# First ada scale on VectorE, 1/rms rows behind the first products, a later scatter, unheld splits at five seams

## The chip, the cores and the metric

One core of one Trainium2 chip runs the program. The metric is the device time of one execution in microseconds (us); lower is better. The kernel computes in single precision: each product of a weight matrix is made of three products of reduced-precision parts (high x high, high x low, low x high), so each weight tile is first split into a high part (a cast on ScalarE, ACT) and a low part (a subtraction on VectorE, DVE).

## The reference, cut to what matters

256 tokens of 1024 features pass through two stacks, one behind the other.

```python
def first_block(x, c, ...):
    for layer in range(2):
        sh1, sc1, g1, sh2, sc2, g2 = split(ada_mod(c, ada_w[layer], ada_b[layer]), 6)   # silu(c) @ w + b
        h = rmsnorm(x, norm_mix_g[layer]) * (1.0 + sc1) + sh1
        y = mlstm_mixer(h, ...) if layer < 1 else stick_breaking_mixer(h, ...)
        x = x + g1 * y
        h = rmsnorm(x, norm_ffn_g[layer]) * (1.0 + sc2) + sh2
        x = x + g2 * peer_ffn(h, ...)          # top 16 of 16384 experts in 8 heads
    return x

def second_block(h, p, ...):
    for i in range(2):
        h = h + 0.5 * swiglu(rms_norm(h, g_ffn1[i]), ffn1_w_in[i], ffn1_w_out[i])
        hn = rms_norm(h, g_mix[i])
        h = h + (mla_mixer(hn, ...) if i == 0 else fox_mixer(hn, ...))
        h = h + 0.5 * swiglu(rms_norm(h, g_ffn2[i]), ffn2_w_in[i], ffn2_w_out[i])
        gate = sigmoid(rms_norm(h, g_ple[i]) @ ple_w_gate[i])
        h = h + gate * (p[i] @ ple_w_proj[i])
    return h
```

## The kernel before, in words

**Stages.** The list at L1731 gives the order: mlstm, peer(0), stick, peer(1), then ffn1_0, mla, ffn2_0 with ple(0), ffn1_1, fox, ffn2_1 with ple(1). A seam is the border between two of them: the residual x is finished there, normalised, transposed and split for the next stage. The program hands instructions to a scheduler that sets the order on each engine by its own estimates. Two things constrain it: `issue_after` (an instruction is issued only behind another; here "hold"), and `pe_order`, in which TensorE's instructions keep the order of the code.

**Start.** `ada_first` (L585) makes the first shift and scale: vectors of 1024, silu(c) times two 1024x1024 blocks of `ada_w`. Eight loads of 1 MB come from SP's queue, first the four of the shift (pool "first"), then the four of the scale (`wpool`, whose four buffers serve all later weights). TensorE multiplies them with `cs` as a one-column stationary operand (L601), the result row is copied (L606), turned into columns of 128 by transposes (L608), and the bias added (L615, L612, L613). Until both are there the transposed, normalised x cannot be scaled and shifted (L332, L334).

**Weights.** `units` and `stream` (L191 to L211) load 128x2048 tiles named raw; `split` (L216) makes whi (L229) and wlo (L230). `lin_s` (L274) makes 24 products of 128x256 from one unit (lines L280 to L282), `lin_m` (L234) products of 128x512 (L244 to L246).

**Late normalisation.** In the second block the products start with the unnormalised x times the gain. `head` transposes x (L306) and splits it (xhi L323, xlo L324); `norm_late` (L402) works out 1/rms on DVE (L408, L346 to L355). Where the 1/rms is wanted along the columns, it multiplies the identity by it (rrt, L422), a product with ones spreads it (L423), and ACT copies the result (rrow, L424). `ffn` (L1150) runs over 22 chunks: gate and up products of one chunk (24 + 24), then sg = gate x rrow (L1182), its silu (L1183), up x rrow (L1184), and the second product two chunks behind. `fox` (L1092) uses the row for its forget gates (L1116 to L1124), whose sums are transposed on TensorE (L1122).

**Seams.** `tail` and `lin_m(tail=True)` write the last products, the evacuations (`residual`: x at L467, L469) and the heads in `pe_order`; then `boundary` (L477) puts up to five holds on the next stage's first splits: the first `free` of them wait for the last addition to x, the others for the last xlo. `free` is 2 for mla and fox, 1 for the ffn stages, and 5 (no hold) from ffn2 to ple. ple(l) evacuates through ACT (L1226) and DVE (L1227, L1228).

**Scatter.** In a peer layer TensorE runs "u phase" units (L1468, 32 products each) while DVE picks the experts. `par(u0, 7, (rt, 15))` at L1589 runs seven units beside the routing; the scatter of the chosen weights starts with products L1360 on ex (L1355). Later in the phase a set of indices passes through jT (L1700).

Of the kernel before, what the change touches and what calls it, by code (L numbers as in the profile page):

```python
# [10 lines left out]
F32 = mybir.dt.float32  # L11
# [6 lines left out]
OP = mybir.AluOpType  # L18
AX = mybir.AxisListType

P = 128
S = 256
D = 1024
NK = D // P
# [91 lines left out]
class Kern:  # L116
    def __init__(self, ctx, tc, I, out):
# [12 lines left out]
        self.early = True  # L130
# [4 lines left out]
        self.free = 1  # L135
# [98 lines left out]
    def lin_m(self, xT, nk, srcs, ncol, evac, tag="acc", blocks=None, tail=False, late=0):  # L234
# [24 lines left out]
        if tail:  # L259
            rest = [(k, next(us)) for k in range(4, nk, kk)]  # L260
            with self.pe_order():
# [7 lines left out]
                if late:  # L269
                    self.holds = [(), self.evac_ins, self.evac_ins]  # L270
                else:
                    self.boundary()
# [129 lines left out]
    def norm_late(self, rows=False, inv=False):  # L402
# [8 lines left out]
        R = None  # L411
        if rows:
            self.uid += 1
            R = self.spool.tile([P, S], F32, tag="rrow", bufs=1, name=f"rrow_{self.uid}")
            ps = self.ps("acc")
            for tb in range(2):
                t = self.spool.tile([P, P], F32, tag="rrt", bufs=2, name=f"rrt_{self.uid}_{tb}")
                r = rs[tb]
                if inv:
                    r = self.small(1, "rms")  # L420
                    nc.vector.reciprocal(r, rs[tb])
                nc.vector.tensor_scalar(t, self.ident, r, None, OP.mult)  # L422
                nc.tensor.matmul(ps[:, tb * P:(tb + 1) * P], self.ones, t, start=True, stop=True)  # L423
            nc.scalar.copy(R, ps[:, 0:S])  # L424
        return hT, rs, R

# [7 lines left out]
    def tail(self, prod, ev, acc):  # L434

        with self.pe_order():
# [13 lines left out]
            self.boundary()  # L450
# [68 lines left out]
    def ada_sum(self, src, bias, out):  # L519
# [4 lines left out]
        sm = self.small(NK, "adsm")  # L524
        for h in range(2):
            ps = self.ps("acc" if self.early else "mm")
# [10 lines left out]
        nc.vector.tensor_add(out, sm, bias)  # L537
# [47 lines left out]
    def ada_first(self):  # L585
# [3 lines left out]
        row = [self.ps("acc") for _ in range(4)]  # L589
        ctx = ExitStack()  # L590
        pool = ctx.enter_context(self.tc.tile_pool(name="first", bufs=4, side="right", reuse_waits="tile"))
        for e in range(2):
            for k0 in range(0, NK, 2):
                self.uid += 1
                raw = (self.wpool if e else pool).tile([P, 2048], F32, tag="raw", bufs=4, name=f"raw_{self.uid}")
                nc.sync.dma_start(raw.rearrange("p (k n) -> p k n", k=2),
                                  self.I["ada_w"][0, k0 * P:(k0 + 2) * P, e * D:(e + 1) * D].rearrange("(k p) n -> p k n", p=P))
                for k in range(k0, k0 + 2):
                    for h in range(2):
# [1283 lines left out]
```

## Time and profile before

| | |
|---|---|
| median of 3 runs | 2852.85 us (2849.33 to 2853.03) |
| profiled execution | 2852.44 us, span 2850.7 us |
| mean granted clock of TensorE | 0.987 of full speed |
| TensorE (PE) | 2754.4 us busy |
| weight loads (PEld), beside PE | 2537.3 us |
| DVE | 1931.0 us |
| ACT | 929.4 us |
| POOL | 433.2 us |
| read from HBM | 743.76 MB, 261 GB/s |

The span is what the profiler saw from the first to the last instruction; the time of the execution is a little longer. Busy times are sums over the span, and say nothing on which engine ends a stage; the waits and the windows do. The granted clock is the share of full speed that TensorE was given in a stretch.

### The profile page before, as it was taken

The numbers are of one execution on the slowest core, as the hardware profiler recorded it, in microseconds if no ns is written. First come the engines' busy times: TensorE is split into PE (matmuls) and PEld (weight loads), VectorE is DVE, ScalarE is ACT, GpSimd is POOL, SyncE is SP. The second block draws the span as 40 slices with busy tenths as digits, with TensorE's granted clock in tenths as the row PEclk, the third lists the DMA queues.
The fourth block names the chain that finished last, engine by engine and source line by source line (L and its number), as shares of the span: only waits on it lengthen the run. The fifth ranks groups of instructions, "written<-read, shape, count | busy, mean of one in ns | idle before, by whom it ended". The sixth has DMA issues, their size and how long they took to land.

```text
span 2850.7 us, 47773 instructions
## 1 busy us (share of the span) xinstructions
PE 2754.4 (97%) x19250; PEld 2537.3 (89%) x19250; DVE 1931.0 (68%) x4005; ACT 929.4 (33%) x1728; POOL 433.2 (15%) x445
## 2 busy tenths in 40 slices
PE   7999999999998999999999998999999999999999
PEld 4789999999998779999999997998799889887998
DVE  4877866768545977867777446667666666666665
ACT  3653111100001664111100003446654554456444
POOL 0000342333332000233443430000000000000000
PEclk9999999999999999999999999999999999999999
DMA  7654999999997724899999996554255545442553
GB/s 263 225 196 167 346 397 356 372 378 384 380 409 310 264 102 147 314 375 415 412 408 407 408 408 244 182 186 154 73 192 192 182 163 192 154 157 92 190 187 113
DMA packets 155582, 747.92 MB, mean 262 GB/s; under 512 B 15696, under 2 KB 17360, under 8 KB 111840
## 3 DMA queue, kind: packets, MB, share of 16 engines
q1 hardware_dynamic: 93984, 527.93, 49.9%
q0 software_dynamic: 58752, 213.94, 19.2%
q10 hardware_dynamic: 2624, 3.00, 0.4%
q8 instruction: 151, 2.47, 0.4%
q14 instruction: 71, 0.58, 0.1%
HBM read 743.76 MB, written 1.05 MB: 261 GB/s over the span
## 4 chain that ended last, share of the span: by engine, by line
PE 68%; DMA 17%; DVE 9%; issue 3%; ACT 2%; POOL 1%; ACTq 0%; DVEq 0%; POOLq 0%
PE ps_acc L1519 11%; PE ps_mm L280 7%; PE ps_mm L282 7%; PE ps_mm L281 7%; PE ps_mm L1468 6%; DMA raw<-in_peer_v_dram 5%; DMA row<-in_peer_un_dram,ix 5%; DMA row<-in_peer_v_dram,ix 4%; PE ps_acc L245 4%; PE ps_acc L244 4%; PE ps_acc L246 4%; PE ps_acc L1161 3%; PE ps_acc L1163 3%; PE ps_acc L1162 3%; DMA row<-in_ada_w_dram 2%
## 5 line engine op out<-in xcount | busy, mean ns | idle before, releaser
L230 DVE TENSOR_TENSOR wlo<-raw,whi 128x1024 fp32r<-128x1024 f32 (+1 forms) x440 | 533.2, 1214 | 237.3 <-ACT whi L229 228.8
L229 ACT CAST whi<-raw 128x1024 fp32r<-128x1024 f32 (+1 forms) x440 | 455.3, 1042 | 509.5 <-PE ps_mm L281 244.4
L1519 PE MATMUL ps_acc<-X,raw 128*128 128x176 f32 (+1 forms) x4096 | 606.4, 308 | 10.4 <-DMA raw<-in_peer_v_dram 10.0
L1468 PE MATMUL ps_mm<-hT,raw 128*128 128x176 f32 (+1 forms) x4096 | 604.6, 309 | 4.5 <-ACT jT L1700 4.3
L1519 PEld LDWEIGHTS ps_acc<-X,raw 128*128 128x128 f32 x4096 | 587.0, 190 | 16.3 <-DMA raw<-in_peer_v_dram 14.9
L1468 PEld LDWEIGHTS ps_mm<-hT,raw 128*128 128x128 f32 x4096 | 590.4, 191 | 6.2 <-ACT jT L1700 4.6
L280 PE MATMUL ps_mm<-xhi,whi 128*128 128x256 f32 (+1 forms) x1488 | 422.7, 284 | 11.4 <-DVE sg L1182 7.4
L281 PE MATMUL ps_mm<-xlo,whi 128*128 128x256 f32 (+1 forms) x1488 | 420.0, 283 | 2.0 <-DVE xlo L324 1.1
L282 PE MATMUL ps_mm<-xhi,wlo 128*128 128x256 f32 (+1 forms) x1488 | 420.0, 283 | 0.3 <-DVE wlo L230 0.3
L1438 DVE SCALAR_TENSOR_TENSOR sacc<-row,dots,sacc 128x1024 f32<-128x1024 f32 x172 | 220.8, 1284 | 146.5 <-DMA row<-in_peer_v_dram,ix 145.9
L280 PEld LDWEIGHTS ps_mm<-xhi,whi 128*128 128x128 f32 (+1 forms) x1488 | 282.7, 190 | 17.0 <-DVE sg L1182 8.3
L1421 DVE SCALAR_TENSOR_TENSOR row<-row,hn 128x1024 f32<-128x1024 f32 x176 | 213.4, 1224 | 113.6 <-DMA row<-in_peer_un_dram,ix 113.3
L1414 POOL DMA_INDIRECT row<-in_peer_un_dram,ix x176 | 199.3, 1132 | 588.0 <-DVE ti L1619 240.1
L281 PEld LDWEIGHTS ps_mm<-xlo,whi 128*128 128x128 f32 (+1 forms) x1488 | 282.3, 190 | 6.3 <-DVE xlo L324 1.8
L282 PEld LDWEIGHTS ps_mm<-xhi,wlo 128*128 128x128 f32 (+1 forms) x1488 | 282.9, 190 | 1.3 <-DVE wlo L230 0.8
L1414 POOL DMA_INDIRECT row<-in_peer_v_dram,ix x176 | 190.1, 1080 | 337.0 <-ACT ix L1411 171.1
L1470 ACT ACTIVATE X<-ps_mm 128x352 f32<-128x352 f32 (+1 forms) x128 | 57.5, 451 | 482.0 <-PE ps_mm L1468 384.9
L1411 ACT CAST ix<-ps_mm 128x4 int32<-128x4 f32 x88 | 14.2, 161 | 492.8 <-PE ps_mm L1408 336.1
L1161 PE MATMUL ps_acc<-whi,ah 128*128 128x512 f32 x352 | 139.3, 396 | 0.0
L1163 PE MATMUL ps_acc<-whi,al 128*128 128x512 f32 x352 | 137.8, 392 | 0.0
L1162 PE MATMUL ps_acc<-wlo,ah 128*128 128x512 f32 x352 | 136.8, 389 | 0.0
L1508 DVE SCALAR_TENSOR_TENSOR X<-ps_mm,X 128x128 f32<-128x128 f32 (+1 forms) x210 | 66.2, 365 | 85.2 <-PE ps_mm L1502 64.3
(466 smaller groups left out, 3764.6 us busy)
## 6 DMA issues: line engine op xcount, KB each, us to landing
raw<-in_ffn_dram SPq DMA_DIRECT2D x132, 1024.0 KB, 4.9
raw<-in_peer_u_dram SPq DMA_DIRECT2D x128, 1024.0 KB, 8.2
raw<-in_peer_v_dram SPq DMA_DIRECT2D x128, 1024.0 KB, 13.1
raw<-in_ada_w_dram SPq DMA_DIRECT2D x28, 1024.0 KB, 5.3
row<-in_ada_w_dram POOLq DMA_DIRECT2D x40, 512.0 KB, 10.4
raw<-in_peer_wq_dram SPq DMA_DIRECT2D x16, 1024.0 KB, 5.5
raw<-in_fox_in_dram SPq DMA_DIRECT2D x12, 1024.0 KB, 5.0
raw<-in_ma_vo_dram SPq DMA_DIRECT2D x8, 1024.0 KB, 5.0
```

Source lines behind the costliest of these rows:

```text
L229: nc.scalar.copy(hi[:, 0:u], raw)
L230: nc.vector.tensor_sub(lo[:, 0:u], raw, hi[:, 0:u])
L280: nc.tensor.matmul(o, wh, xh[:, k, :], start=(k == 0), stop=False)
L281: nc.tensor.matmul(o, wh, xl[:, k, :], start=False, stop=False)
L282: self.last_mm = nc.tensor.matmul(o, wl, xh[:, k, :], start=False, stop=(k == NK - 1))
L1161: nc.tensor.matmul(o, ah[:, t], wh[:, n], start=(c == 0), stop=False)
L1162: nc.tensor.matmul(o, ah[:, t], wl[:, n], start=False, stop=False)
L1163: nc.tensor.matmul(o, al[:, t], wh[:, n], start=False, stop=(c == FFC - 1))
L1414: nc.gpsimd.indirect_dma_start(row, None, src, bass.IndirectOffsetOnAxis(held["ix"][:, k:k + 1], 0))
L1438: nc.vector.scalar_tensor_tensor(sacc[u], row, w, sacc[u], OP.mult, OP.add)
L1468: self.last_mm = nc.tensor.matmul(ps[:, i * TD:(i + 1) * TD], raw[:, o:o + P], hT[:, k, TS:S], start=(k == 0), stop=(k == NK - 1))
L1519: self.last_mm = nc.tensor.matmul(o, w, xs[:, 0, :], start=(first and c % 2 == 0), stop=last, skip_group_check=True)
```

## The change

Four things change. (1) In `ada_first` the four scale loads and the four shift loads alternate; the scale is worked out on DVE, one multiplication and seven multiply-adds of 128x1024, and the sums over partitions are made by eight transposes, a reduction on DVE and four accumulating copies on ACT (`col_sums`, split from `ada_sum`); the shift stays on TensorE. (2) `as_rows` holds the code that spreads 1/rms: in `ffn` it comes behind the last product of chunk 0, and the accumulators are allocated behind it; in `fox` it comes with the gates at the first evacuation of q. (3) In layer 1 one more u phase unit runs before the scatter, and one less behind it. (4) `boundary` is gone: splits are no longer held at the seams ffn1_0 to mla, mla to ffn2_0, ple(0) to ffn1_1, ffn1_1 to fox and fox to ffn2_1. The holds from peer(1) to ffn1_0 stay.

```diff
 def ada_first(self):
-        row = [self.ps("acc") for _ in range(4)]
+        w = self.I["ada_w"]
+        row = [self.ps("acc") for _ in range(2)]
+        acc = self.bpool.tile([P, D], F32, tag="ada", bufs=1, name="ada_first")
...
-        for e in range(2):
-            for k0 in range(0, NK, 2):
...
+        for k0 in range(0, NK, 2):
+            raw = load(pool, k0, 1)
+            for k in range(k0, k0 + 2):
+                r = raw[:, (k - k0) * D:(k - k0 + 1) * D]
+                if k == 0:
+                    nc.vector.tensor_scalar(acc, r, self.cs[:, 0:1], None, OP.mult)
+                else:
+                    nc.vector.scalar_tensor_tensor(acc, r, self.cs[:, k:k + 1], acc, OP.mult, OP.add)
+            raw = load(self.wpool, k0, 0)
+            for k in range(k0, k0 + 2):
+                for h in range(2):
+                    o = (k - k0) * D + h * 512
+                    nc.tensor.matmul(row[h][0:1, :], self.cs[:, k:k + 1], raw[:, o:o + 512], start=(k == 0),
+                                     stop=(k == NK - 1))
+        sc = self.small(NK, "adas")
+        self.col_sums(acc, sc, "acc")
+        nc.vector.tensor_add(sc, sc, self.col("ada_b0", 8, 8))
...
+    def as_rows(self, rs, inv=False, after=None):
...
+            nc.vector.tensor_scalar(t, self.ident, r, None, OP.mult)
+            with ExitStack() as hold:
+                if after is not None:
+                    hold.enter_context(self.tc.issue_after(after.ins))
                 nc.tensor.matmul(ps[:, tb * P:(tb + 1) * P], self.ones, t, start=True, stop=True)
...
 def ffn(self, src, mid=None):
-            hT, _, R = self.norm_late(rows=True)
-            acc = [self.ps("acc") for _ in range(4)]
+            hT, rs, _ = self.norm_late()
...
                 self.lin_s(hT, uh, ul, P, pu[:, 0:S])
+                if c == 0:
+                    R = self.as_rows(rs, after=self.last_mm)
+                    acc = [self.ps("acc") for _ in range(4)]
...
 fox, ev(dst, gain, dT):
+                    if dst is q and nb + tb == 0:
+                        gate()
                     nc.scalar.copy(d3[tb], p3)
...
-    def boundary(self):
-
-        if self.gain is not None:
-            self.holds = [] if self.free == 5 else [(self.add_ins,)] * self.free + [self.evac_ins] * (5 - self.free)
...
-                        self.boundary()
+                        self.holds = [(self.add_ins,)] + [self.evac_ins] * 4
...
-            par(u0, 7, (rt, 15))
+            par(u0, 7 + l, (rt, 15))
             next(u0)
-            par(u0, half - 8, (rt, 28), (f, c0), (extra, 6 if l == 0 else 0))
+            par(u0, half - 8 - l, (rt, 28), (f, c0), (extra, 6 if l == 0 else 0))
```

In the changed kernel line numbers shift: L601 becomes L614, L608 L625, L306 L302, L334 L330, L280 to L282 become L276 to L278, L229 and L230 become L227 and L228, L422 L421, L423 L425, L424 L426, L1182 L1198, L1226 to L1228 become L1241 to L1243.

The first place is the end of `ada_first` on TensorE. Before (115 and 116 are the two halves of the scale's row, 113 and 114 those of the shift):

```order
L601 MATMUL ps_acc_116<-raw_176,cs 1x512
L601 MATMUL ps_acc_115<-raw_176,cs 1x512
L601 MATMUL ps_acc_116<-raw_176,cs 1x512
L608 MATMUL ps_acc_182<-consts,row_183 128x1 x4
L608 MATMUL ps_acc_182<-consts,row_189 128x1 x4
L280 MATMUL ps_mm_311<-xhi_253,whi_307 128x256
```

Now, with ada_first the accumulator that DVE fills and raw_143 and raw_153 the last two shift loads:

```order
L614 MATMUL ps_acc_113<-raw_143,cs 1x512
L614 MATMUL ps_acc_114<-raw_143,cs 1x512
L530 MATMUL ps_acc_160<-consts,ada_first 128x128 x4
L530 MATMUL ps_acc_166<-consts,ada_first 128x128 x4
L614 MATMUL ps_acc_113<-raw_153,cs 1x512
L614 MATMUL ps_acc_114<-raw_153,cs 1x512
L614 MATMUL ps_acc_113<-raw_153,cs 1x512
L614 MATMUL ps_acc_114<-raw_153,cs 1x512
L625 MATMUL ps_acc_113<-consts,row_178 128x1 x4
L625 MATMUL ps_acc_113<-consts,row_184 128x1 x4
L276 MATMUL ps_mm_304<-xhi_246,whi_300 128x256
```

The eight transposes of the scale's accumulator now stand ahead of the last four products of the shift.

The second place is the start of ffn1_1 on TensorE: before, the spreading products stand behind chunk 1 (96 products) and directly ahead of chunk 2 (ps_mm_20062).

```order
L281 MATMUL ps_mm_19993<-xlo_19822,whi_19988 128x256
L282 MATMUL ps_mm_19993<-xhi_19821,wlo_19989 128x256
L423 MATMUL ps_acc_19900<-rrt_0_19901,consts 128x128
L423 MATMUL ps_acc_19900<-rrt_1_19904,consts 128x128
L280 MATMUL ps_mm_20062<-xhi_19821,whi_20054 128x256
```

Now they stand behind chunk 0 (48 products), ahead of chunk 1 (ps_mm_19985):

```order
L277 MATMUL ps_mm_19903<-xlo_19815,whi_19898 128x256
L278 MATMUL ps_mm_19903<-xhi_19814,wlo_19899 128x256
L425 MATMUL ps_acc_19953<-rrt_0_19954,consts 128x128
L425 MATMUL ps_acc_19953<-rrt_1_19957,consts 128x128
L276 MATMUL ps_mm_19985<-xhi_19814,whi_19977 128x256
```

In ffn2_0 and ffn2_1 they moved from behind 96 products to behind 73, in fox from behind the 24 products of the gates to behind those and the first 48 of lin_m, and in ffn1_0 they did not move.

The third place is the same seam, ple(0) to ffn1_1, on ACT, between the second evacuation of ple and the last of x's split. Before:

```order
L1226 ACTIVATE tsp_19749<-ps_acc_19674,st_19656 128x512
L229 CAST whi_19914<-raw_19912 128x1024
L361 ACTIVATE sqj_19747,pt_19672<-x_84 128x512
L361 ACTIVATE sqj_19753,pt_19672<-x_85 128x512
L1226 ACTIVATE tsp_19815<-ps_acc_19755,st_19656 128x512
L323 ACTIVATE xhi_19821<-ps_mm_19823,cols 128x256
L323 ACTIVATE xhi_19821<-ps_mm_19832,cols 128x256
L323 ACTIVATE xhi_19821<-ps_mm_19823,cols 128x256
L323 ACTIVATE xhi_19821<-ps_mm_19832,cols 128x256
L361 ACTIVATE sqj_19819,pt_19672<-x_84 128x512
L1226 ACTIVATE tsp_19853<-ps_acc_19756,st_19656 128x512
```

Now:

```order
L357 ACTIVATE sqj_19746,pt_19665<-x_85 128x512
L227 CAST whi_19977<-raw_19975 128x1024
L1241 ACTIVATE tsp_19808<-ps_acc_19748,st_19649 128x512
L319 ACTIVATE xhi_19814<-ps_mm_19816,cols 128x256
L319 ACTIVATE xhi_19814<-ps_mm_19825,cols 128x256
L319 ACTIVATE xhi_19814<-ps_mm_19816,cols 128x256
L227 CAST whi_19981<-raw_19975 128x1024
L319 ACTIVATE xhi_19814<-ps_mm_19825,cols 128x256
L357 ACTIVATE sqj_19812,pt_19665<-x_84 128x512
L1241 ACTIVATE tsp_19846<-ps_acc_19749,st_19649 128x512
L227 CAST whi_20047<-raw_20045 128x1024
L357 ACTIVATE sqj_19850,pt_19665<-x_85 128x512
```

Three casts that stood behind all of these now stand among them. On DVE the steps of 1/rms (L408 to L422) stood between the subtractions of six splits, and now follow each other with at most an xlo between two.

## Rows read from the trace of the kernel before

**Rows 1.** The page: busy time of each engine over the whole span.

```profile
PE 2754.4 (97%) x19250; PEld 2537.3 (89%) x19250; DVE 1931.0 (68%) x4005; ACT 929.4 (33%) x1728; POOL 433.2 (15%) x445
```

**Rows 2.** TensorE's waits, whole span: waiter, releaser, us in total, times, longest.

```profile
PE ps_mm L280 <- DVE sg L1182: 7.4, 4, 2.2
PE ps_acc L423 <- DVE rrt L422: 6.9, 2, 4.5
PE ps_mm L1360 <- ACT ex L1355: 6.5, 2, 4.6
...
PE ps_mm L1468 <- ACT jT L1700: 4.3, 1, 4.3
...
PE ps_mm L688 <- DVE u L679: 2.4, 1, 2.4
...
PE ps_mm L306 <- DVE x L1228: 2.1, 1, 2.1
```

**Rows 3.** Windows: length, TensorE busy, clock, DMA share, GB/s; last row ACT's timeline.

```profile
69.20:74.50 5.30, 5.30 (x32) 0.68 0.24 65
1155.10:1161.00 5.90, 5.89 (x21) 0.61 0.00 0
1229.60:1237.00 7.40, 7.37 (x36) 0.65 0.56 180
...
1226.26 0.22 ACT L1425 ACTIVATE dots<-dots 128x16 f32<-128x16 f32 x1 [9.65 <-DVE row L1421]
```

**Rows 4.** Windows behind L423: ffn2_0, ffn1_1, fox, ffn2_1.

```profile
2081.70:2087.00 5.30, 5.30 (x45) 1.00 0.26 107
2305.10:2310.00 4.90, 4.90 (x29) 0.66 0.23 87
2490.50:2494.70 4.20, 4.20 (x13) 0.59 0.91 335
2640.40:2645.00 4.60, 4.60 (x26) 0.63 0.32 134
```

**Rows 5.** Chain of waits, first 46 us: start, us, what.

```profile
8.78 19.35 PE ps_acc L601 x40
...
28.46 1.02 PE ps_mm L306 x8
...
38.14 3.54 PE ps_acc L601 x8
...
43.28 0.03 DVE tsp L334
```

**Rows 6.** Window of the loads: length, PE, PEld, DVE, ACT, POOL, clock, DMA, GB/s.

```profile
8.50:28.20 19.70, 19.42 (x42) 3.59 (x43) 5.91 (x26) 3.68 (x11) 0.00 (x0) 1.00 1.00 389
```

**Rows 7.** The ada_w loads, and DVE's multiply-add (ns min/median/max).

```profile
0.75 15.52 SPq L596 DMA_DIRECT2D raw<-in_ada_w_dram  x8
DMA to landing us min/median/max: 10.6/11.7/15.9
L510 DVE SCALAR_TENSOR_TENSOR ada<-raw,cs,ada x21: 1265/1279/1286, 58.8 to 158.3; 128x1024 f32<-128x1024 f32 x21
```

**Rows 8.** Timeline of ple(0) and ffn1_1: TensorE at L423, ACT at L1226.

```profile
2302.30 0.61 PE L423 MATMUL ps_acc<-rrt,consts 128*128 128x128 f32 x4
2305.07 0.38 PE L280 MATMUL ps_mm<-xhi,whi 128*128 128x256 f32 x1 [2.17 <-DVE sg L1182]
2305.29 0.28 PE L281 MATMUL ps_mm<-xlo,whi 128*128 128x256 f32 x1
2305.41 0.28 PE L282 MATMUL ps_mm<-xhi,wlo 128*128 128x256 f32 x1
...
2282.63 0.69 ACT L1226 ACTIVATE tsp<-ps_acc,st 128x512 f32<-128x512 f32 x1 [3.74 <-PE ps_acc L246]
```

**Rows 9.** The page: the subtractions and casts of the splits, us in all, mean ns.

```profile
L230 DVE TENSOR_TENSOR wlo<-raw,whi 128x1024 fp32r<-128x1024 f32 (+1 forms) x440 | 533.2, 1214 | 237.3 <-ACT whi L229 228.8
L229 ACT CAST whi<-raw 128x1024 fp32r<-128x1024 f32 (+1 forms) x440 | 455.3, 1042 | 509.5 <-PE ps_mm L281 244.4
```

More of the change, by code (lines that the diff above doesn't have):

```diff
@@ L410, in norm_late @@
         rs = [st[:, 2 + tb:3 + tb] for tb in range(2)]
[L411 to L422, printed above, removed]
+        return hT, rs, self.as_rows(rs, inv) if rows else None
+    def as_rows(self, rs, inv=False, after=None):
+        nc = self.nc
+        self.uid += 1
+        R = self.spool.tile([P, S], F32, tag="rrow", bufs=1, name=f"rrow_{self.uid}")
+        ps = self.ps("acc")
+        for tb in range(2):
+            t = self.spool.tile([P, P], F32, tag="rrt", bufs=2, name=f"rrt_{self.uid}_{tb}")
+            r = rs[tb]
+            if inv:
+                r = self.small(1, "rms")
+                nc.vector.reciprocal(r, rs[tb])
+            nc.vector.tensor_scalar(t, self.ident, r, None, OP.mult)
+            with ExitStack() as hold:
+                if after is not None:
+                    hold.enter_context(self.tc.issue_after(after.ins))
                 nc.tensor.matmul(ps[:, tb * P:(tb + 1) * P], self.ones, t, start=True, stop=True)
-            nc.scalar.copy(R, ps[:, 0:S])
-        return hT, rs, R
+        nc.scalar.copy(R, ps[:, 0:S])
+        return R
     def norm_T(self, gain, shift=None, dst=None):
@@ new lines, in load @@
+        def load(pl, k0, e):
+            self.uid += 1
+            raw = pl.tile([P, 2048], F32, tag="raw", bufs=4, name=f"raw_{self.uid}")
+            nc.sync.dma_start(raw.rearrange("p (k n) -> p k n", k=2),
+                              w[0, k0 * P:(k0 + 2) * P, e * D:(e + 1) * D].rearrange("(k p) n -> p k n", p=P))
+            return raw
+        for k0 in range(0, NK, 2):
[12 more added lines that the diff above has]
+                                     stop=(k == NK - 1))
@@ new lines, in ada_first @@
+        sc = self.small(NK, "adas")
+        self.col_sums(acc, sc, "acc")
+        nc.vector.tensor_add(sc, sc, self.col("ada_b0", 8, 8))
+        nc.vector.scalar_tensor_tensor(m["a1"], sc, 1.0, self.col("norm_mix_g0"), OP.add, OP.mult)
+        ps = row[0]
+        for h in range(2):
+            t = pool.tile([P, 512], F32, tag=f"row{h}", bufs=1, name=f"row{h}")
+            (nc.vector.tensor_copy if h else nc.scalar.copy)(t[0:1, :], row[h][0:1, :])
+            for c in range(4):
+                nc.tensor.transpose(ps[:, h * 4 + c:h * 4 + c + 1], t[0:1, c * P:(c + 1) * P], self.ident[0:1, 0:1])
@@ L616, in ada_first @@
+        nc.vector.tensor_add(m["sh1"], ps[:, 0:NK], self.col("ada_b0", 0, 8))
         ctx.close()
@@ L1195, in ffn_ple @@
             self.gain, self.dst = self.col(f"g_ple_{l}"), self.yT_tiles(pl)
-            free, self.free = self.free, 5
             self.ffn(self.I["ffn2"][l])
-            self.gain, self.free = nxt, free
+            self.gain = nxt
             self.ple(l)
@@ L1743, in run @@
         for i, (s, *_) in enumerate(stages):
-            _, nxt, *free = stages[i + 1] if i + 1 < len(stages) else (None, None)
+            nxt = stages[i + 1][1] if i + 1 < len(stages) else None
             self.gain = col(nxt) if nxt else None
-            self.free = free[0] if free else 1
             s()
```

65 lines of the change are left out of this document (21 added, 44 removed).

## Prediction, made before the changed kernel ran

> **What bounds the kernel now.** I read the page first, then the waits of TensorE, then the windows around each wait. TensorE is busy 97% of the span and DVE 68% [rows 1]: only some 96 us of the span are free of products, and an edit pays if it shortens those idle stretches, the half-speed stretches that follow them, or TensorE work itself. The list of waits says where they are [rows 2]: the start, the waits on sg (L1182), on rrt (L422), on ex (L1355), on jT (L1700) and on x at the seams. The windows show the second cost: a stretch of some 2 to 5 us without products is mostly followed by 4 to 8 us at a granted clock near 0.6, that is partly at 1.2 instead of 2.4 GHz [rows 3, 4]. The loss there is taken as the length times (1 - clock). All sums below are against the profiled execution, 2852.44 us with a span of 2850.7; the median of the runs is 2852.85, 0.4 above it.
>
> **Part A, the first scale on VectorE.** Until 43.28 nothing can be normalised with scale and shift: TensorE works through L601 from 8.78, and 1.6 us lie between the end of its last piece and tsp (L334): a row copy, transposes, two small adds [rows 5]. L601 has 64 records, 40 of which take 19.35 us and the last 8 take 3.54, 0.44 to 0.48 each [rows 5]. The loads are not the bound: the eight ada_w loads are issued by 16.3 and take a median 11.7 us to land, and from 8.5 to 28.2 the queues run at 389 GB/s [rows 6, 7]. I put the landing of the last raw at 27.9, an estimate from these rows (16.3 + 11.7).
> After the change half of L601 goes (32 records, some 14 us of TensorE) and DVE gets eight products of at most 1.28 (L510's time), 10.2 us in a stretch of 19.7 in which it is busy 5.9 [rows 6, 7]. They follow the loads. The end is then: last scale load, one before the last raw, at 27.9 - 2.7 (1.05 MB at 389 GB/s) = 25.2; two products, 27.8; eight transposes, 1.0 as L306 x8, 28.8; these stand in TensorE's order ahead of the last four shift products, whose 8 records take 3.5: 32.3, or 32.4 with the issue gaps; then the same 1.6 as now: L334 at 34.0 instead of 43.28. That is -9.2. The reduce and the four ACT accumulations of the scale run beside the last shift products.
> Against it stands that TensorE now waits for each shift load: two loads or 5.4 us apart with 3.5 us of work. The rows show what such a pause costs later: after an idle 2.2 at L1182, 4.6 to 4.9 us at 0.63 to 0.66, a loss of 1.7 [rows 4]. So I take -9.2 + 1.7 = **-7.5**. Bounds: -9.2 (no drop) and -3.8 (the last 5.4 us of TensorE work, 1.0 + 3.5 + the transposes of the rows, some 0.9, all at half speed).
> [...]
> DVE's own next work (x's normalisation, L388) is interleaved with the products and ready long before 27.9. The wpool buffers come free earlier, so ma_qk is loaded behind the ada loads and earlier than now; I cost that at nothing, since one load feeds 48 products, 5.8 us at 0.12 from start to start [rows 8], and takes 2.7.
> In the gates behind it (L688 waits 2.4 on u, then 5.3 us at 0.68, 4.1 in all [rows 2, 3]) the order of the DVE chain changes: u now stands behind fewer splits. L688 too stands earlier on TensorE. Bounds 0 and -4.1; I take **-1.5**, nearer to nothing as both ends of the wait move.
>
> **Part B, rows of 1/rms behind the first products.** In an ffn stage before, rrt and L423 stand after the 96 products of chunks 0 and 1, and chunk 2 needs PSUM that only sg frees. In ffn1_1 L423 starts at 2302.30 and L280 goes on at 2305.07: in these 2.8 us stand L423 itself, the copy of rrow, sg on DVE behind a split, and 2.17 of idle [rows 8]. All four stages have it, 7.4 us in all [rows 2]. After the change L425 comes behind chunk 0 in ffn1_1, with 96 products after it (11.5 us at 0.12 from start to start [rows 8]), and in both ffn2 about 24 products of chunk 1 remain (2.9 us). The chain of 2.8 us fits behind them. Gain: ffn2_0 2.2 (clock 1.00 after it, nothing more); ffn1_1 2.2 + 4.9 x 0.34 = 3.8; ffn2_1 2.2 + 4.6 x 0.37 = 3.9 [rows 4].
> In fox L423 waited 2.4 on rrt (6.9 less ffn1_0's 4.5 [rows 2]) and the next 4.2 us ran at 0.59 [rows 4]: 2.4 + 1.7 = 4.1. Now rrt is written before the splits, and L425 stands behind the first 48 products of lin_m. The gate's chain (L624 to L634) has 55 products of lin_m before the transposes that need it, where it had 43 before and they waited for nothing, so nothing is late there.
> In ffn1_0 L423 waits 4.5 on rrt and L280 0.9 on sg (the rest of the 7.4) [rows 2], 5.4 in all. Its rrt is held back by the rotary arithmetic and eight splits on DVE, and the order there stays as it was, L423 behind 96 products: **0**, although it is the largest of these waits. Part B: **-14.0**; bounds -16.7 (half of ffn1_0's too) and -9 (idle gained, clock not).
>
> **Part C, one more u phase unit before the scatter in layer 1.** L1360 waits 4.6 on ex and the next 5.9 us run at 0.61: 6.9 in all [rows 2, 3]. Another unit's 32 products fill it. But the unit is taken from later, where TensorE waits 4.3 on jT and then runs 7.4 us at 0.65 [rows 2, 3], and the order still has 23 units before that point. DVE's expert chain sets jT; it is not shortened, and only the lost clock and a slightly earlier start of the chain come back. Bounds 0 and -6.9; **-2**, nearer to nothing.
>
> **Part D, splits no longer held at five seams.** The first two or three casts (1.04 each on ACT) and subtractions (1.21 on DVE [rows 9]) now stand between the evacuations that the seam waits for: at ple(0) to ffn1_1 one cast stands ahead of the second L1241 on ACT and one subtraction between xlo's. TensorE waits there 2.1 on x already [rows 2]. Price: between nothing and one cast and one subtraction, 2.3, at each; I take 0.6, x 5 = **+3.0**. What they release (first products earlier) is nothing beyond part B: the list has no long wait on whi or wlo at the seams.
>
> **Sum.** -7.5 - 1.5 - 14.0 - 2.0 + 3.0 = -22.0: 2830.4 for the profiled execution, 2830.8 against the median. Predicted 2831.
>
> **The rivals.**
> - The clock at the start (part A gives 3.8): -18.3, 2834.5. For it: every idle stretch over 2 us but one is followed by a drop [rows 4]. Against: the 16 transposes of x, 2 us, fill one pause. Chance 0.15.
> - The scatter's gain is whole, because ACT and DVE finish the chain of jT earlier by what the scatter saves: 4.9 more, 2826. For it: ACT is idle before the later stall [rows 3]. Against: ACT waits there for DVE's expert rows, 9.65 [rows 3]. Chance 0.1.
> - The seams take back part B: each unheld split delays an evacuation by 2.3 us and every second seam loses 1.8 of clock, 5 x 2.3 + 3 x 1.8 = 17 instead of 3. Then 2845. Chance 0.12.
> - Slower: the same mechanism stronger, casts in ACT's queue ahead of the evacuations. If two casts and a subtraction, 3.3, stand in front of x at each of the five seams and each is followed by a drop of 1.8, that is 25.5, and rrt is late again, so part B's 14 are gone: -11 + 25.5 = +14.5, 2867. It decides the sign from some 2.2 us a seam with B gone. Against: ACT idles 3.74 ahead of L1226 and has room for such casts [rows 8]. Chance 0.04.
> - Part B doesn't do what it says outside ffn1_0 either: the hold keeps L425 behind chunk 0, but if rrt is late there (as in ffn1_0) TensorE waits earlier instead, and the 14 become about 5: 2840. Chance 0.12.
>
> **How the numbers follow.** The forecast has 0.47: with its own bounds 2826 to 2836. The range 2820 to 2844 takes in the rivals of 2826 to 2840. About 0.2% or 5.7 us is what a measurement of this kernel can tell from no change, so "same" is 2847 to 2858.5. Faster 0.89 (all but the last part of the seam rival and the slower one), same 0.06, slower 0.05.
>
> **What would show it.** L601's successor L614 has 32 records; tsp (now L330) starts near 34 (33 to 40). No wait of L276 on sg in ffn2_0, ffn1_1 and ffn2_1, no wait of L425 in fox, and a clock of 1.00 after them; ffn1_0's wait of 4.5 still there. At the scatter the wait on ex near nothing, and the one on jT as long or longer. The waits of L302 on x a little longer than before (L306's). It is wrong if tsp starts after 40, if the clock falls to 0.5 before 34, if new waits on x of 3 us stand at the seams, or if the DVE is late with rrt.

## The result and the profile after

The changed kernel takes 2827.1 us (median of four executions, 2823.03 to 2828.77) where the kernel before took 2852.94 beside it: a ratio of 0.9913, interval 0.9898 to 0.9929. By the medians 25.8 us are gone; 22 were forecast, and the range of 2820 to 2844 holds the time. The profiled execution is one of the four, 2825.78 against 2852.44 before, 26.7 less. One of the six executions of e9_old_start below took 6345.98 us; its ratio is over the other five.

The page of the changed kernel, its first rows, to be laid beside [rows 1]:

```profile
span 2824.0 us, 47731 instructions
...
PE 2729.4 (97%) x19218; PEld 2527.1 (89%) x19218; DVE 1938.8 (69%) x4013; ACT 927.3 (33%) x1735; POOL 435.5 (15%) x445
```

TensorE has 32 records fewer and 25.0 us less of busy time; DVE has 7.8 more. TensorE's share is still 97%: its busy time and the span fell together.

TensorE's waits in the changed kernel, whole span, columns as in [rows 2]:

```profile
PE ps_acc L614 <- DMA raw<-in_ada_w_dram: 13.0, 2, 12.4
...
PE ps_mm L1483 <- ACT ix L1426: 4.3, 1, 4.3
PE ps_mm L560 <- DVE ada L558: 4.3, 1, 4.3
PE ps_acc L425 <- DVE rrt L421: 4.3, 1, 4.3
PE ps_mm L530 <- DVE ada L490: 4.3, 2, 3.1
...
PE ps_mm L302 <- DVE x L1243: 2.6, 1, 2.6
...
PE ps_mm L1375 <- ACT ex L1370: 2.1, 2, 1.9
...
PE ps_mm L1483 <- DVE X L1523: 2.0, 1, 2.0
...
PE ps_mm L276 <- DVE sg L1198: 0.9, 1, 0.9
```

Of the 7.4 on sg [rows 2] only ffn1_0's 0.9 is left, of the two waits on rrt only ffn1_0's, and the wait on ex at the scatter (4.6 in layer 1) has shrunk to 0.2; the 1.9 here is layer 0's. What stood on jT (4.3) now stands on ix, at the same products and as long. The seam's wait on x rose from 2.1 to 2.6. TensorE's windows in the changed kernel, columns as in [rows 4]; the first three lie in the start, the fourth in layer 0, the last four around or just behind the rows product (L425) of ffn2_0, ffn1_1, fox and ffn2_1:

```profile
12.00:18.00 6.00, 5.39 (x8) 1.00 1.03 355
28.00:34.00 6.00, 4.95 (x20) 1.00 1.03 425
37.00:45.00 8.00, 7.50 (x40) 0.60 0.34 104
415.00:420.00 5.00, 0.68 (x2) 0.88 1.02 418
2064.00:2074.00 10.00, 10.00 (x88) 1.00 0.56 211
2288.00:2292.00 4.00, 4.00 (x36) 1.00 0.60 197
2472.00:2490.00 18.00, 18.00 (x86) 1.00 0.63 224
2609.00:2622.00 13.00, 13.00 (x109) 1.00 0.43 163
```

The drops of [rows 4] are gone: 1.00 in all four. A drop behind the wait on x at ple(0) to ffn1_1 stays: 0.83 from 2272 to 2282, and 0.83 from 2285 to 2295 in the kernel before. The start of the changed kernel on TensorE (start, us, instruction, idle before and what ended it):

```profile
12.39 5.39 PE L614 MATMUL ps_acc<-raw,cs 128*1 128x512 f32 x8 [12.39 <-DMA raw<-in_ada_w_dram]
18.41 3.59 PE L614 MATMUL ps_acc<-raw,cs 128*1 128x512 f32 x8 [0.63 <-DMA raw<-in_ada_w_dram]
21.93 1.97 PE L302 MATMUL ps_mm<-consts,rawn 128*128 128x128 f32 x16
23.83 3.59 PE L614 MATMUL ps_acc<-raw,cs 128*1 128x512 f32 x8
28.81 1.09 PE L530 MATMUL ps_acc<-consts,ada_first 128*128 128x128 f32 x8 [1.39 <-DVE ada_first L609]
29.83 3.59 PE L614 MATMUL ps_acc<-raw,cs 128*1 128x512 f32 x8
...
36.61 0.58 PE L276 MATMUL ps_mm<-xhi,whi 128*128 128x256 f32 x1 [2.01 <-ACT xhi L333]
```

and DVE's tsp behind it:

```profile
34.91 0.99 DVE L330 TENSOR_SCALAR tsp<-ps_mm,a,sh 128x256 f32<-128x256 f32 x2
```

tsp starts at 34.91 (43.28 before [rows 5]) and the first product at 36.61 (45.0 before), 8.4 earlier. How far the changed kernel is ahead, point by point of the program, in the two profiled executions (a table product is one of those at L1502, now L1517, that spread the chosen weights over the experts; the expert phase of layer 0 is taken from the first of them to the first transpose of the layer's output, oT):

| point | ahead by, us |
|---|---|
| first product | 8.4 |
| transposes of mlstm's output gate, layer 0 | 10.5 |
| first table product of layer 0 | 10.5 |
| end of layer 0's expert phase | 0.4 |
| end of layer 1's expert phase | 6.6 |
| end of fox's attention | 22.2 |
| end | 26.7 |

Two things in it were not foreseen: the start's gain vanishes in layer 0 and comes back in part in layer 1, and the second block gives 20 us.

### The profile page after: what moved, and what is told of

Same layout as the page of the kernel before. It is cut to its first block, busy times and chain, and to the rows that moved or that the text cites. A ratio compares the mean times of both kernels' runs of the same rounds, so it can differ in the third digit from the quotient of the medians.

```text
span 2824.0 us, 47731 instructions
## 1 busy us (share of the span) xinstructions
PE 2729.4 (97%) x19218; PEld 2527.1 (89%) x19218; DVE 1938.8 (69%) x4013; ACT 927.3 (33%) x1735; POOL 435.5 (15%) x445
## 4 chain that ended last, share of the span: by engine, by line
PE 72%; DMA 14%; DVE 7%; issue 3%; ACT 1%; POOL 0%; DVEq 0%; POOLq 0%; SPq 0%; ACTq 0%
PE ps_acc L1534 12%; PE ps_mm L1483 11%; PE ps_mm L276 7%; PE ps_mm L278 7%; PE ps_mm L277 7%; PE ps_acc L243 4%; PE ps_acc L242 4%; PE ps_acc L244 4%; DMA raw<-in_peer_v_dram 4%; DMA row<-in_peer_v_dram,ix 3%; DMA row<-in_peer_un_dram,ix 3%; PE ps_acc L1174 3%; PE ps_acc L1176 3%; PE ps_acc L1175 3%; DMA row<-in_ada_w_dram 2%
## 5 line engine op out<-in xcount | busy, mean ns | idle before, releaser
L228 DVE TENSOR_TENSOR wlo<-raw,whi 128x1024 fp32r<-128x1024 f32 (+1 forms) x440 | 532.9, 1214 | 239.6 <-ACT whi L227 231.4
L227 ACT CAST whi<-raw 128x1024 fp32r<-128x1024 f32 (+1 forms) x440 | 456.8, 1043 | 500.6 <-PE ps_mm L277 237.3
L276 PE MATMUL ps_mm<-xhi,whi 128*128 128x256 f32 (+1 forms) x1488 | 418.7, 282 | 5.4 <-ACT xhi L333 2.0
L278 PE MATMUL ps_mm<-xhi,wlo 128*128 128x256 f32 (+1 forms) x1488 | 417.1, 281 | 1.2 <-DVE wlo L228 1.2
L276 PEld LDWEIGHTS ps_mm<-xhi,whi 128*128 128x128 f32 (+1 forms) x1488 | 279.8, 188 | 10.2 <-ACT xhi L333 2.1
L278 PEld LDWEIGHTS ps_mm<-xhi,wlo 128*128 128x128 f32 (+1 forms) x1488 | 280.6, 189 | 2.4 <-DVE wlo L228 1.9
L1426 ACT CAST ix<-ps_mm 128x4 int32<-128x4 f32 x88 | 14.2, 161 | 492.6 <-PE ps_mm L1423 374.4
```

What stands on the lines that cost most here:

```text
L227: nc.scalar.copy(hi[:, 0:u], raw)
L228: nc.vector.tensor_sub(lo[:, 0:u], raw, hi[:, 0:u])
L276: nc.tensor.matmul(o, wh, xh[:, k, :], start=(k == 0), stop=False)
L278: self.last_mm = nc.tensor.matmul(o, wl, xh[:, k, :], start=False, stop=(k == NK - 1))
```

## The experiments

Each ran beside the kernel before on the same chip; "gain" is (1 - ratio) times the median of the kernel before.

| kernel | ratio, interval | gain, us |
|---|---|---|
| e1_first_scale | 0.9967, 0.9953 to 0.9981 | 9.4 |
| e2_rows_late | 0.9982, 0.9971 to 0.9994 | 5.1 |
| e3_scatter_later | 0.9998, 0.9985 to 1.001 | 0.6 |
| e4_no_holds | 0.9955, 0.9942 to 0.9968 | 12.8 |
| e5_change_again | 0.9901, 0.9883 to 0.9919 | 28.3 |
| e6_no_ffn_rows | 0.9887, 0.9868 to 0.9905 | 32.3 |
| e7_shift_first | 0.9889, 0.9868 to 0.991 | 31.7 |
| e8_ffn1_0_free | 0.9883, 0.9864 to 0.9901 | 33.4 |
| e9_old_start | 0.9922, 0.9907 to 0.9937 | 22.2 |
| e10_no_scatter | 0.9898, 0.9882 to 0.9914 | 29.1 |
| e11_rotary_later | 0.9878, 0.9862 to 0.9893 | 34.8 |
| e12_rotary_no_ffn_rows | 0.9863, 0.9847 to 0.9878 | 39.1 |

**The four parts alone.** The first four put one part each into the kernel before.

e1_first_scale has the new `ada_first` and `col_sums`, part A:

```diff
 def ada_first(self):
+            raw = load(pool, k0, 1)
...
+                    nc.vector.scalar_tensor_tensor(acc, r, self.cs[:, k:k + 1], acc, OP.mult, OP.add)
+            raw = load(self.wpool, k0, 0)
...
+        self.col_sums(acc, sc, "acc")
```

> The kernel before with the first scale on VectorE alone. Theory: the start saves 8 us and the gates behind it 2 more (first product near 36.6 instead of 45.0, scatter products of layer 0 near 270.7 instead of 281.1), and the expert phase of layer 0 gives nearly all of it back, since TensorE there waits for the background rows of ada_w that arrive through queues at over 400 GB/s: the end of that phase (oT's first product) stays within 2 us of 904.2, total 2850 to 2853. Rival: the loss in layer 0 came from orders that the other parts changed; then the end of the phase is near 894 and the total near 2842.

Measured: 9.4 us, the first product at 36.6, as in the whole change. The loss in layer 0 did not come again: its expert phase took 492.9 us here, against 499.7 in the changed kernel and 489.6 before, with the same order of instructions as in the changed kernel. So the 10 us are no fixed price of the early start; whether it costs a part of them is taken up below.

e2_rows_late has `as_rows` and its two new places, part B:

```diff
-            hT, _, R = self.norm_late(rows=True)
-            acc = [self.ps("acc") for _ in range(4)]
+            hT, rs, _ = self.norm_late()
...
+                if c == 0:
+                    R = self.as_rows(rs, after=self.last_mm)
+                    acc = [self.ps("acc") for _ in range(4)]
```

> The kernel before with the rows of 1/rms behind the first products alone, holds kept. Theory: the waits on sg in ffn2_0, ffn1_1 and ffn2_1 (2.2 each and two clock drops) and on rrt in fox (2.4 and a drop) go: -10 to -14, 2839 to 2843. Rival: rrt comes early only when the splits are not held at the seams, so that alone the product of rows waits for rrt behind chunk 0: half or less of it, 2846 or more.

Measured: 5.1 us, and only fox's wait on rrt is gone. In ffn1_1 the rows product still stands behind the 96 products. TensorE of e2_rows_late there:

```profile
2302.20 0.28 PE L282 MATMUL ps_mm<-xhi,wlo 128*128 128x256 f32 x1
2302.32 0.60 PE L429 MATMUL ps_acc<-rrt,consts 128*128 128x128 f32 x4
2305.09 0.38 PE L280 MATMUL ps_mm<-xhi,whi 128*128 128x256 f32 x1 [2.17 <-DVE sg L1194]
```

These are the rows of before, to a few hundredths [rows 8]. DVE in e2_rows_late tells why (the chain of 1/rms runs from L408 to rrt, L425):

```profile
2289.58 0.15 DVE L408 TENSOR_TENSOR st<-pt 128x2 f32<-128x2 f32 x1
...
2292.16 1.23 DVE L230 TENSOR_TENSOR wlo<-raw,whi 128x1024 fp32r<-128x1024 f32 x1
2293.31 0.15 DVE L353 TENSOR_TENSOR nw<-st 128x2 f32<-128x2 f32 x1
2293.38 1.22 DVE L230 TENSOR_TENSOR wlo<-raw,whi 128x1024 fp32r<-128x1024 f32 x1
...
2299.53 0.48 DVE L425 TENSOR_SCALAR rrt<-consts,st 128x128 f32<-128x128 f32 x2
```

Between each two of the last seven small steps of the chain stands a held split's subtraction of 1.2 us, six in all, and rrt comes 10.0 us after L408. The new place in the code only lets the rows product stand behind chunk 0; with rrt this late the scheduler leaves it where it was, behind 96 products in all four ffn stages.

e3_scatter_later has part C:

```diff
-            par(u0, 7, (rt, 15))
+            par(u0, 7 + l, (rt, 15))
             next(u0)
-            par(u0, half - 8, (rt, 28), (f, c0), (extra, 6 if l == 0 else 0))
+            par(u0, half - 8 - l, (rt, 28), (f, c0), (extra, 6 if l == 0 else 0))
```

> The kernel before with one more unit ahead of the scatter in layer 1 alone. Theory: the wait of 4.6 on ex and its clock drop go, the later stall of 4.3 stays but comes 7 us earlier, and the phase of the second table product by queues near 410 GB/s keeps it: -5 to -7, 2846 to 2848. Rival: the unit is only moved and the phase that is bound by its loads ends when it did: -2 at most, 2851 or more.

Measured: nothing that shows (0.9998; the interval runs from 4.3 us gained to 2.9 lost). Layer 1's wait on ex fell from 4.6 to 0.2, and TensorE waits later instead (TensorE's waits, whole span; both stand in layer 1):

```profile
PE ps_mm L1468 <- DVE X L1508: 4.0, 1, 4.0
...
PE ps_mm L1468 <- ACT ix L1411: 3.1, 1, 3.1
```

All of TensorE's waits from before the scatter to behind that place (1110 to 1350) sum to 7.7 here and 8.9 before.

e4_no_holds has part D:

```diff
                 if late:
                     self.holds = [(), self.evac_ins, self.evac_ins]
-                else:
-                    self.boundary()
...
             self.head(1)
-            self.boundary()
...
-                        self.boundary()
+                        self.holds = [(self.add_ins,)] + [self.evac_ins] * 4
```

> The kernel before without the holds at the five seams alone. Theory: the waits on xlo at fox and on whi at the seams go, rrt is early, and x is late by 0.5 at ple's seam only: -2 to -6, 2847 to 2851; the waits on sg of 2.2 stay. Rival, as predicted: casts and subtractions ahead of the evacuations cost 0.6 a seam, +3, 2856.

Measured: 12.8 us, the largest of the four, where a loss of 3 had been forecast. The waits on sg in ffn2_0, ffn1_1 and ffn2_1 are gone although the rows code is the old one. The same chain on DVE in e4_no_holds (L406 is its first step, L420 writes rrt):

```profile
2284.06 1.22 DVE L230 TENSOR_TENSOR wlo<-raw,whi 128x1024 fp32r<-128x1024 f32 x1
2285.19 0.15 DVE L406 TENSOR_TENSOR st<-pt 128x2 f32<-128x2 f32 x1
...
2288.70 0.16 DVE L353 SCALAR_TENSOR_TENSOR st<-nw,st 128x2 f32<-128x2 f32 x1
2288.89 0.16 DVE L351 TENSOR_TENSOR nw<-st 128x2 f32<-128x2 f32 x1
2289.09 0.16 DVE L352 TENSOR_TENSOR nw<-nw,nw 128x2 f32<-128x2 f32 x1
2289.28 0.16 DVE L353 SCALAR_TENSOR_TENSOR st<-nw,st 128x2 f32<-128x2 f32 x1
2289.48 0.48 DVE L420 TENSOR_SCALAR rrt<-consts,st 128x128 f32<-128x128 f32 x2
```

rrt comes 4.3 us after L406 instead of 10.0: the first splits were made earlier, between the evacuations, and none stands in the chain. TensorE in e4_no_holds at that seam:

```profile
2284.20 1.76 PE L304 MATMUL ps_mm<-consts,x 128*128 128x128 f32 x7 [2.64 <-DVE x L1225]
2285.61 0.56 PE L278 MATMUL ps_mm<-xhi,whi 128*128 128x256 f32 x1
...
2291.71 0.61 PE L421 MATMUL ps_acc<-rrt,consts 128*128 128x128 f32 x4
```

The scheduler now puts the rows product 6.1 us behind the first product; in e2_rows_late these were 13.0 (2289.32 to 2302.32). With the old rows code it stands behind 73, 45 and 73 products in ffn2_0, ffn1_1 and ffn2_1, instead of 96. The cost that was feared is there too, but small: the wait on x is 2.64 where it was 2.1 [rows 2]. In fox the wait on rrt is gone as well, but two new ones on xlo, in front of its first products, take its place, so that D alone gains nothing there:

```profile
PE ps_mm L279 <- DVE xlo L322: 3.0, 2, 1.7
```

What A to D gave alone sums to 9.4 + 5.1 + 0.6 + 12.8 = 27.9; the whole change gave 28.3 in e5_change_again and, by its ratio, 24.8 in the first comparison. In the second block, here taken from ffn1_0's first second product to the last product of ple(1), the addition holds in the trace: it took 1067.25 us before, 1060.93 in e2_rows_late (6.3 less), 1053.95 in e4_no_holds (13.3 less), and 1047.53 in the changed kernel, 19.7 less where 6.3 + 13.3 makes 19.6. By stages, each from the first transposes of its seam; a "start" ends at the stage's first second product, the others at the next seam:

| stage, us | before | B alone | D alone | changed |
|---|---|---|---|---|
| start of ffn1_0 | 30.8 | | | 30.5 |
| mla | 116.2 | 115.4 | 113.8 | 113.8 |
| start of ffn2_0 | 26.6 | 28.2 | 23.3 | 23.3 |
| ple(0) and ffn1_1 | 224.9 | 224.8 | 221.2 | 221.0 |
| fox | 140.7 | 135.0 | 141.4 | 135.1 |
| start of ffn2_1 | 27.9 | 26.6 | 23.3 | 23.3 |

B's 28.2 and 26.6 are not its own: e1_first_scale, with neither part, has 28.1 and 26.6 there. The wait on sg of 2.2 stands in both starts in all three kernels, but the lower clock followed it in one only, and not always the same: before in ffn2_1 [rows 4], in e2_rows_late in ffn2_0 (its windows behind the two waits):

```profile
2080.40:2085.00 4.60, 4.60 (x27) 0.63 0.25 103
2635.00:2639.60 4.60, 4.60 (x39) 1.00 0.25 103
```

**The change again, and with one thing taken out.** e5_change_again is the changed kernel without an edit, for the spread of its phases.

> The changed kernel once more, for where its gain stands. In its first profile the 10.5 us won by the start of layer 0's expert phase were lost again inside it (489.6 us before, 499.7 after, from the first table product to oT), and the second expert phase was 6 shorter. Theory: these phases vary from run to run by some 5 us with the order in which their transfers land, and the kernels with one part each took 492 to 493: this profile has 490 to 496 in the first phase, the start's 10 us are still there behind it, and the time is 25 to 30 below the kernel before. Rival: the phase gives the start's gain back whenever it comes early: 498 or more again.

Measured: 28.3 us; the profiled execution took 2819.38. The second block is the same, 1047.5; layer 0's expert phase took 495.7.

e6_no_ffn_rows takes the ffn part of B out of the change:

```diff
-            hT, rs, _ = self.norm_late()
+            hT, rs, R = self.norm_late(rows=True)
+            acc = [self.ps("acc") for _ in range(4)]
...
-                if c == 0:
-                    R = self.as_rows(rs, after=self.last_mm)
-                    acc = [self.ps("acc") for _ in range(4)]
```

> The changed kernel, with the rows of 1/rms in the four ffn stages back in their old place in the code (ahead of chunk 0), those of fox left where the change put them. Theory: without the holds on the splits the scheduler puts the rows behind 48 to 73 products by itself, so the waits on sg stay away and the time is that of the changed kernel within 2 us. Rival, as predicted: the waits on sg of 2.2 come back in ffn2_0, ffn1_1 and ffn2_1 with two clock drops, 8 to 10 us slower than the changed kernel.

Measured: 0.9887, within the interval of the change, second block 1047.8. The rows behind chunk 0 are worth nothing in the ffn stages once the holds are gone; of part B only fox counts.

e7_shift_first undoes the alternation of the loads, the scale staying on DVE:

```diff
         for k0 in range(0, NK, 2):
-            raw = load(pool, k0, 1)
+            raw = load(pool, k0, 0)
...
+        for k0 in range(0, NK, 2):
+            raw = load(self.wpool, k0, 1)
```

> The changed kernel with the four shift loads first and the four scale loads behind them, the scale still on VectorE. Theory: the end of the start is set by the last load and DVE's two last products; tsp comes at 27.9 + 2.6 + transposes 1.0 + reduce 0.7 + accumulations about 1 = 33 to 34.5, as with alternating loads (34.9), first product 36 to 37, time equal within 1 us. Rival: TensorE finishes its products near 21, idles and is throttled, so transposes and first products run at half speed: first product 38 or later, 3 us slower.

Measured: the first product at 38.8 instead of 36.6, yet no loss in the time (0.9889 against 0.9901, the intervals overlap widely). TensorE in e7_shift_first:

```profile
8.75 16.14 PE L607 MATMUL ps_acc<-raw,cs 128*1 128x512 f32 x32 [8.75 <-ACT cs L1725]
...
33.46 1.97 PE L530 MATMUL ps_acc<-consts,ada_first 128*128 128x128 f32 x8 [6.09 <-DVE ada_first L616]
38.80 0.58 PE L276 MATMUL ps_mm<-xhi,whi 128*128 128x256 f32 x1 [3.37 <-ACT xhi L333]
```

TensorE has its half done at 24.9, makes the transposes of x and of the shift, then idles 6.09 for the last scale products on DVE, and the eight transposes of the scale take 1.97 instead of 1.09. The window of these transposes in the same kernel shows the granted clock at 0.50, the lower level of 1.2 GHz:

```profile
33.40:35.50 2.10, 1.97 (x8) 0.50 1.00 414
```

e9_old_start is the changed kernel with the old `ada_first`:

```diff
-        for k0 in range(0, NK, 2):
-            raw = load(pool, k0, 1)
...
+        for e in range(2):
+            for k0 in range(0, NK, 2):
```

> The changed kernel with the old start (first scale on TensorE, its loads behind the shift's). Theory: the start is worth 8.5 us at the first product and 10.5 behind the gates, and the expert phase of layer 0 takes 3 to 5 us longer when it begins earlier (496 us on average in six profiles with the new start, 492 in four with the old one): 5 to 8 us slower than the changed kernel, with layer 0's phase at 490 to 493. Rival: the phase's length has nothing to do with the start; 9 to 11 us slower.

Measured: 22.2 us of gain. Taking part A out costs 6.1 against e5_change_again and 2.6 against the first comparison; the intervals (0.9907 to 0.9937 here, 0.9883 to 0.9919 and 0.9898 to 0.9929 there) overlap, so by the times A's worth in company is between about nothing and the 9.4 that it has alone. Layer 0's expert phase took 496.5 without the early start, longer than in any other kernel with the old one.

e10_no_scatter is the changed kernel with the old numbers of part C:

```diff
-            par(u0, 7 + l, (rt, 15))
+            par(u0, 7, (rt, 15))
             next(u0)
-            par(u0, half - 8 - l, (rt, 28), (f, c0), (extra, 6 if l == 0 else 0))
+            par(u0, half - 8, (rt, 28), (f, c0), (extra, 6 if l == 0 else 0))
```

> The changed kernel with the scatter of layer 1 where it was. Theory: the scatter is worth nothing in the end (alone it gave a ratio of 0.9998): the wait of 4.6 on ex and its drop come back, and the phase behind it, whose queues run at 408 GB/s to its end, ends when it did; within 3 us of the changed kernel. Rival: 5 to 7 us slower, as the first profile's wait and drop add up to.

Measured: 0.9898, the same as with C. TensorE's waits in e10_no_scatter; of the first 4.6 stand in layer 1, as do the other two:

```profile
PE ps_mm L1382 <- ACT ex L1377: 6.5, 2, 4.6
...
PE ps_mm L1490 <- DVE X L1530: 2.1, 1, 2.1
```

With jT's 0.9 layer 1's waits from 1110 to 1350 sum to 7.6; in the changed kernel to 6.5, in e5_change_again to 6.2. Over all the profiled kernels this sum is 6.7 to 8.9 in the five without C and 6.2 to 8.7 in the nine with it: the stall moves, and that it gets shorter is not shown.

**The wait that the change leaves.** ffn1_0 still waits 4.3 on rrt and 0.9 on sg. In it `mid`, the rotary arithmetic of mla, is written at chunk 8, and the scheduler pulls it forward on DVE, in front of the chain of 1/rms. Two kernels queue it behind the last subtraction of the chunk before; e8_ffn1_0_free also takes away the holds at the seam from peer(1) to ffn1_0.

```diff
                 if c == 8 and mid is not None:
-                    mid()
+                    with self.tc.issue_after(self.al_ins.ins):
+                        mid()
...
-                nc.vector.tensor_sub(al, up, ah)
+                self.al_ins = nc.vector.tensor_sub(al, up, ah)
...
-                        self.holds = [(self.add_ins,)] + [self.evac_ins] * 4
+                        self.holds = []
```

> The changed kernel with the splits unheld at the sixth seam too (peer of layer 1 to ffn1_0) and the rotary arithmetic queued behind chunk 7 on DVE. Theory: rrt no longer stands behind eight subtractions and the rotary steps, so the wait of 4.3 on rrt and 0.9 on sg and the clock drop behind them go, 8 us together: 2817 to 2821. Rival: casts and subtractions ahead of the last evacuations of the expert layer make x late there by as much: no change or slower.

Measured: the wait on rrt is gone, but TensorE of e8_ffn1_0_free waits at the seam itself:

```profile
1743.05 0.45 PE L302 MATMUL ps_mm<-consts,x 128*128 128x128 f32 x1 [4.31 <-DVE x L475]
```

From the seam to the second product ffn1_0 takes 27.7 us instead of 30.4. Here a split without a hold does what part D was feared to do: it delays x.

e11_rotary_later has the same edit without the last hunk: the holds at that seam stay.

> The changed kernel with the rotary arithmetic queued behind chunk 1's last subtraction on DVE, the holds at peer to ffn1_0 kept. Theory: the rotary steps, not the held splits, make rrt late: the wait on rrt falls from 4.3 to under 1, a wait on sg of up to 2.2 stays, 3 to 6 us faster than the changed kernel, and x at that seam isn't later than now (1.2). Rival: DVE's subtractions alone keep rrt as late; wait over 3, no gain.

Measured: 0.9878. (The subtraction in question is chunk 7's, not chunk 1's: the first rotary step runs at 1806, long behind chunk 1.) No wait on rrt, no new one on x, and of sg 1.82 in place of 0.9; the same stretch takes 26.1 us, 4.4 less than with the change.

e12_rotary_no_ffn_rows is e11_rotary_later with the rows of the ffn stages back in their old place:

```diff
-            hT, rs, _ = self.norm_late()
+            hT, rs, R = self.norm_late(rows=True)
+            acc = [self.ps("acc") for _ in range(4)]
...
-                if c == 0:
-                    R = self.as_rows(rs, after=self.last_mm)
-                    acc = [self.ps("acc") for _ in range(4)]
```

> The changed kernel with the rows of 1/rms of the ffn stages in their old place and the rotary arithmetic queued later: the version that the runs so far point to. Theory: as the rotary step alone, 3 to 6 us faster than the changed kernel, since the place of the rows is worth nothing: 2818 to 2822 where the changed kernel has 2825. Rival: the hold of the rows is needed once rrt is early; slower than with it by 2 or more.

Measured: 2813.01 us, 0.9863. The upper end of its interval, 0.9878, lies below the lower ends of both comparisons of the change (0.9883 and 0.9898): by these ratios, each taken against the kernel before and not side by side, this version beats both kernels, by 39.1 us the one before. Against e11_rotary_later it can't be told apart; each of the two edits alone leaves an interval that overlaps with the change's, both together don't.

**Layer 0's expert phase.** In the profiled executions it took, in us: before 489.6; e1 to e4 492.9, 493.2, 492.6 and 492.4; the change 499.7; e5 to e8 495.7, 499.4, 497.2 and 493.3; e9 to e12 496.5, 498.8, 493.2 and 499.4. Layer 1's, taken from the transposes of hT at its head to the last of oT, took 651.4 before and 642.0 to 647.3 in all others. The kernel before thus shows the shortest of the one and the longest of the other, and the 10 us that the changed kernel lost in layer 0 and the 6 it won in layer 1 lie for the most part in this spread. In the changed kernel's trace 8.6 us of the phase are waits on ada, work of the background ada rows (L560 and L530 in the list of waits above), where the kernel before has 2.9; in front of one of them the DMA queues moved 418 GB/s (the window of 415 to 420 above). That wait in the changed kernel, and in its place before:

```profile
419.40 2.04 PE L560 MATMUL ps_mm<-ada,consts 128*128 128x512 f32 x2 [4.32 <-DVE ada L558]
...
427.75 1.52 PE L559 MATMUL ps_mm<-ada,consts 128*128 128x512 f32 x3 [2.21 <-DVE ada L557]
```

Whether the early start lengthens the phase is open. The eight kernels with the alternating loads average 496.6 (492.9 to 499.7), the five with the old start 492.9 (489.6 to 496.5); the ranges overlap, and DVE's order in the phase differs a little between the two groups too. On average the eight are ahead of the five by 8.8 us at the first product, 12.8 at the first table product and 9.1 at the phase's end: close to the 9.4 that part A gave alone.

## Why the prediction was right, and for which wrong reasons

The time was right. Two terms were right in place and size, and two were credited to the wrong part.

- **A, forecast -7.5 and -1.5 at the gates.** Right in mechanism and nearly in size. The transposes of the scale were to end at 28.8 and started at 28.81, 1.0 late; the shift products behind them end at 33.4 (forecast 32.4), tsp follows 1.5 later (1.6) at 34.91 (34.0). Hence -8.4 at the first product where -9.2 was the sum without a drop (its own times, 43.28 and 34.0, make 9.3; two more of the sums are off by 0.1 in the same way). The term of +1.7 for a drop was not needed: TensorE idled 0.63 and 1.39 between its bursts, and the clock stayed at 1.00 from 12 to 34. The fall to 0.60 from 37 to 45 comes behind the last 2.5 us of waits (2.01 on xhi and 0.51 on xlo) and was there before, 0.57 from 46 to 54. The Trainium skill, page TensorE: Matmul & The Clock Gate, section "HAM oscillation — how this bites in real kernels", tells of a kernel that was throttled at every burst of products, where each wait for a transfer was longer than the burst before it. The changed start is not that case: its waits between bursts, 0.63 and 1.39, are shorter than the bursts of 3.59. The trace of e7_shift_first agrees with the Trainium skill in kind, though the wait there is for DVE: behind 6.09 us of idle the transposes ran at 0.50. The rival of a drop at the start also leaned on "every idle stretch over 2 us but one" being followed by a drop; in the whole trace before there is another without one, 2.21 at 427.75 with 1.00 behind it. From the first product to mlstm's output gate 2.1 more were won (10.5 - 8.4), for a forecast of 1.5 at the gates; the wait on u there is 0.2 where it was 2.4 [rows 2]. Alone, A is worth 9.4 (5.4 to 13.4 by its interval) of the 9.0 forecast.
- **B, forecast -14.0.** Wrong in the step that said that this part brings the product behind chunk 0 in the ffn stages. It gave 5.1 in the time and 6.3 in the second block, nearly all of it in fox (5.7 for a forecast of 4.1). For the three ffn stages, with B alone, the last rival was right in its size (5) and in its cause, a late rrt; only, TensorE does not wait earlier, the rows product stays behind 96 products. A hold sets only how early it may stand. The order of the changed kernel, with all four parts in it, showed the rows product early, and I credited that to the part that moves its code.
- **C, forecast -2.** Not seen in the time and, with an interval from -4.3 to +2.9, not excluded either. The wait on ex went as said, and TensorE waits later instead, as the prediction argued: DVE's and ACT's chain to the second place is not shortened.
- **D, forecast +3.0.** Wrong in sign: -12.8 alone. The price at the seam was right where it could be seen (0.5 at ple(0), forecast 0.6). What was missed is what the held splits did behind the seam: they stood in the chain of 1/rms, six times 1.2 us. Freed, they bring the starts of ffn2_0, ffn1_1 and ffn2_1 3.3, 3.7 and 4.5 forward, against the 2.2, 3.8 and 3.9 that I had put down to B; mla gains 2.4, which nothing in the prediction gives. The four kernels with the holds take 115.4 to 116.3 there, the ten without them 113.6 to 114.6. A part is clock: it was 0.57 from 2013 to 2017 in the kernel before, and 1.00 there in e4_no_holds (2005 to 2020) and the changed kernel (2000 to 2020). How the released splits bring that about stays open.
- **ffn1_0, forecast 0.** Right: the wait on rrt is 4.3 (4.5 before).

So the sum came out, by luck, from one error against another: B was 14.0 - 5.1 too large, D too small by 12.8 + 3.0, and of C's 2 nothing was seen. The second block alone gave 20 where B and D together were to give 11. The seam rival (17 us of new waits) was wrong: at no seam that the change touches did a wait on x exceed 2.64.

## What to carry to other kernels

A hold that keeps work away from one short wait puts that work somewhere: look at which chain it then stands in, and who waits at that chain's end. When several edits move one order, run (or order) each alone before a term is credited to it; an order made by all of them tells what moved, not which edit moved it. And lay a gain or loss within one phase beside that phase's spread over several executions before it is explained.

## What was not expected of the hardware

Layer 0's expert phase, in which the queues move 376 to 383 GB/s and are busy 97 to 99% of the time (changed kernel and kernel before), took 499.7 and 495.7 us in two profiled executions of the changed kernel, and 492.9 in e1_first_scale with the same order in it. The second block stayed within 1046.2 to 1048.7 in all nine profiled kernels with both B's fox part and D. In the start of the changed kernel the clock stayed at 1.00 behind idle of 0.63 and 1.39; behind 6.09 in e7_shift_first eight transposes took 1.97 at 0.50 instead of 1.09. In between it is no matter of the length alone: behind the same wait of 2.2 on sg, in the same stage, the clock was 1.00 in one kernel and 0.63 in the other.
